# Moving the softmax's negated maximum to VectorE and the turning of queries and keys to ScalarE copies, in a two-layer diffusion step

## The chip, the core and the metric

The kernel runs on one core of one Trainium2 chip. A core has five engines with instruction queues of their own: TensorE (PE: matmuls, with PEld for its weight loads), VectorE (DVE), ScalarE (ACT), GpSimd (POOL) and SyncE (SP, which issues nearly all transfers here). The metric is the device time of one execution in microseconds (us): 2378.9 us median of three runs before the change.

## The reference

One inference step of a backbone with two layers, width 2048, for two groups of 128 tokens (context and latents). All arithmetic is fp32. Layer 0 mixes with eight heads of latent attention (A) and eight of grouped-query attention with normalised queries and keys (B); layer 1 mixes with eight heads of differential attention (C); each layer is followed by a gated ConvFFN of width 5632. What the change touches:

```
def rmsnorm(x, g):
    y = xf * lax.rsqrt(jnp.mean(xf * xf, axis=-1, keepdims=True) + EPS)
    return (y * g.astype(jnp.float32)).astype(x.dtype)

def apply_rope(x, cos, sin):
    x1, x2 = x[..., :half], x[..., half:]
    return jnp.concatenate([x1 * c - x2 * s, x1 * s + x2 * c], axis=-1)

def diff_attention(q, k, v, lam, scale):      # in each block of 128 queries
    s = jnp.einsum("bqhjd,bkhjd->bhjqk", qb, k).astype(jnp.float32) * scale
    p = jax.nn.softmax(s, axis=-1)
    a = (p[:, :, 0] - lam * p[:, :, 1]).astype(v.dtype)
    return jnp.einsum("bhqk,bkhd->bqhd", a, v)
```

Context queries see 128 context keys; latent queries see 128 cached and 128 latent keys besides, in one softmax. In C each head has two query and key halves, two softmaxes, and a norm over the head's 256 outputs times a constant.

## The kernel before

Activations lie with features on the 128 partitions and both groups' 256 tokens along the row. Every weight matrix is read once, in transfers of 1 MB (`raw`). Each is split in two parts: ACT rounds it to `wh` (L219), DVE takes the rest as `wl` (L220), and PE multiplies three times per 128x128 block: `wh` with the high and the low part of the activations (L312, L313; L298, L299 where three chunks run side by side) and `wl` with the high part (L316; L300). An output chunk of 128 features from 2048 is 48 such matmuls into one PSUM bank (`acc`, three banks). So PE, ACT and DVE all work on every weight.

The stages in order: input projection of layer 0; the heads of A and B, two per turn, beside their own weights; output projection; ConvFFN 0; then layer 1's input projection with the C heads in between, output projection `w_out_c`, ConvFFN 1.

Beside all this runs the adaLN product, 1 MB tiles `araw` of `w_ada` in two buffers. A unit of four tiles is summed either on PE (16 matmuls of 512 columns, L426, then ACT's copy `am` L368 and four transposes L375) or, for the units listed in `SUMMED`, on DVE: two instructions per tile (`junk`, L403), one per token group, each with the sum read out to `mod`. `pump(rate)` spreads these steps over the chunks. Two buffers mean that a third tile's transfer is issued when the first tile has been used.

The code is written as coroutines: `start` runs one to its first `yield`, and each `pump` lets all go one step on. The order on each engine is made from this program by a scheduler; instructions in it are then issued in order, engine by engine.

Softmax of an AB head (`head_ab`): scores to PSUM, two maxima on DVE (`mx`, L592, L593), the negated maximum times the scale on POOL (`nmx`, L597 and L598), two exponentials on ACT with their sums (`p`, L600), reciprocal and two multiplications on DVE (L624 to L626), three transposes on PE (L607), ACT's copy `pT` (L609), three matmuls with the values. A C head (`attend`) does this twice (`dmx`, POOL's L595), then DVE forms `drec` (L939), `nl` = minus lambda over the second sum (L941), multiplies the second softmax by `nl` (L943) and adds the first (L945); after the values (L952 to L954) come squares on ACT (L958), `var` on POOL (L961, the power at L963, a constant at L964), `on` on DVE (L967), four transposes (L974) and the split into `oall` (L219, L220), the input of the output projection.

A C head's `project` takes four chunks for queries and keys and two for values. For each query or key chunk ACT copies the bank to `dev` (L908) and the context tokens on to `dq` or `dk` (L909), and DVE turns the latent tokens with the helper `rope`: two products on 64 partitions crosswise (L583), one with the cosine (L585), one sum (L586).

`rstd` adds EPS on DVE (L183) and raises to the power -1/2 on POOL (L186); two of its callers then multiply by a scale on POOL (L676, L814). The residual `x` takes each output chunk on DVE (L568).

## Time and profile before

| | us |
|---|---|
| three runs | 2378.08, 2378.9, 2380.63 |
| the profiled execution | 2380.3 |
| its span (first to last instruction) | 2378.5 |
| PE busy | 2314.3 (97%) |
| DVE busy | 1810.0 (76%) |
| ACT busy | 1158.0 (49%) |
| POOL busy | 170.3 (7%) |

The profiled execution lies 1.4 us over the median of the runs and inside their spread. Times in the rows of the trace are microseconds from the start of the span; a busy share is an average over stages that have different limits, so a row for a stretch of the span says more than the table. In that count of stages the C heads run from about 1210 to 1550 us, `w_out_c` to about 1623 and the modulation of the second ConvFFN's input to about 1641.

### The profile page before, as it was taken

To read this page: it belongs to the slowest core of one execution; us is meant where nothing else is said; L and a number is where in the kernel's file an instruction comes from. 1 tells how busy PE (TensorE), PEld (TensorE's weight loads), DVE (VectorE), ACT (ScalarE), POOL (GpSimd) and SP (SyncE) were. 2 spreads that over 40 slices of the span, in tenths; PEclk is the share of its full clock that TensorE was granted. 3 is DMA by queue.
4 is the path that set the end of the run, shared out by engine and by line. 5 is a ranking of instruction groups with operands and counts; after the bars stand their busy time and mean duration, and the time that the engine had idled before them with its cause. 6 is when DMAs were issued, how large, how long until landed. Compare 5 with 4: busy or idle time off the path is not lost.

```text
span 2378.5 us, 47144 instructions
## 1 busy us (share of the span) xinstructions
PE 2314.3 (97%) x19626; PEld 2193.4 (92%) x19626; DVE 1810.0 (76%) x2685; ACT 1158.0 (49%) x1807; POOL 170.3 (7%) x205
## 2 busy tenths in 40 slices
PE   8899999999999999999999999998999999999997
PEld 6778868889999999999989999796999999999997
DVE  2667544479999999999979989898899755666654
ACT  4345544365554345554455554345555534555542
POOL 0002101110000000001220001122000000000011
PEclk9999999999999999999999999898999999999999
DMA  9886677777767877777867787686677555555553
GB/s 372 348 345 243 239 269 280 301 295 259 261 252 283 299 275 257 266 266 261 306 227 247 278 305 288 259 295 247 249 254 262 211 195 195 193 192 192 192 193 120
DMA packets 92405, 610.81 MB, mean 257 GB/s; under 512 B 9952, under 2 KB 17824, under 8 KB 20512
## 3 DMA queue, kind: packets, MB, share of 16 engines
q1 hardware_dynamic: 92192, 607.80, 69.6%
q8 instruction: 154, 2.52, 0.4%
q14 instruction: 59, 0.48, 0.1%
HBM read 603.01 MB, written 4.75 MB: 256 GB/s over the span
## 4 chain that ended last, share of the span: by engine, by line
PE 89%; DVE 5%; DMA 2%; issue 2%; ACT 1%; POOL 0%; POOLq 0%; DVEq 0%; ACTq 0%
PE acc L312 27%; PE acc L316 27%; PE acc L313 26%; PE ada L426 3%; DMA araw<-w_ada 2%; DVE junk L403 2%; DVE wl L220 2%; PE att L617 1%; PE acc L298 1%; PE acc L299 1%; PE acc L300 1%; PE misc L426 0%; PE ada L339 0%; DVE nt L515 0%; PE att L933 0%
## 5 line engine op out<-in xcount | busy, mean ns | idle before, releaser
L219 ACT CAST wh<-raw 128x1024 fp32r<-128x1024 f32 (+1 forms) x788 | 793.5, 1013 | 934.7 <-PE acc L313 765.4
L220 DVE TENSOR_TENSOR wl<-raw,wh 128x1024 fp32r<-128x1024 f32 (+1 forms) x788 | 922.0, 1185 | 344.5 <-ACT wh L219 329.5
L312 PE MATMUL acc<-hx,wh 128*128 128x256 f32 x4064 | 1130.0, 279 | 9.0 <-ACT wh L219 4.2
L316 PE MATMUL acc<-hx,wl 128*128 128x256 f32 x4064 | 1127.4, 278 | 0.9 <-DVE wl L220 0.9
L313 PE MATMUL acc<-hx,wh 128*128 128x256 f32 x4064 | 1127.0, 278 | 0.0
L312 PEld LDWEIGHTS acc<-hx,wh 128*128 128x128 f32 x4064 | 763.6, 188 | 34.2 <-issue 11.8
L316 PEld LDWEIGHTS acc<-hx,wl 128*128 128x128 f32 x4064 | 764.8, 188 | 10.3 <-issue 7.0
L313 PEld LDWEIGHTS acc<-hx,wh 128*128 128x128 f32 x4064 | 764.7, 188 | 8.8 <-issue 7.9
L403 DVE CUSTOM_DVE_ANT_0 junk<-araw,condb 128x2048 f32<-128x2048 f32 (+1 forms) x184 | 424.8, 2309 | 1.0 <-DMA araw<-w_ada 1.0
L313 PE MATMUL acc<-g,wh 128*128 128x256 f32 x1408 | 388.3, 276 | 0.0
L316 PE MATMUL acc<-g,wl 128*128 128x256 f32 x1408 | 388.0, 276 | 0.0
L312 PE MATMUL acc<-g,wh 128*128 128x256 f32 x1408 | 387.8, 276 | 0.0
L313 PEld LDWEIGHTS acc<-g,wh 128*128 128x128 f32 x1408 | 264.3, 188 | 0.0
L316 PEld LDWEIGHTS acc<-g,wl 128*128 128x128 f32 x1408 | 264.1, 188 | 0.0
L312 PEld LDWEIGHTS acc<-g,wh 128*128 128x128 f32 x1408 | 264.0, 188 | 0.0
L175 POOL TENSOR_TENSOR sqacc<-sqacc,sq 128x256 f32<-128x256 f32 x62 | 80.6, 1300 | 1528.0 <-issue 1218.9
L1012 ACT ACTIVATE cv<-acc,convw 128x256 f32<-128x256 f32 x176 | 98.3, 558 | 3.8 <-PE acc L300 3.8
L568 DVE SCALAR_TENSOR_TENSOR x<-acc,mod,x 128x128 f32<-128x128 f32 x192 | 58.0, 343 | 50.5 <-PE acc L316 49.6
L426 PE MATMUL ada<-araw,condw 128*32 128x512 f32 x608 | 83.6, 627 | 4.7 <-DMA araw<-w_ada 3.0
L1018 DVE SCALAR_TENSOR_TENSOR cv<-acc,convw,cv 128x254 f32<-128x254 f32 x176 | 84.2, 479 | 3.6
L1015 DVE SCALAR_TENSOR_TENSOR cv<-acc,convw,cv 128x254 f32<-128x254 f32 x176 | 83.5, 474 | 2.7 <-ACT cv L1012 2.7
L316 PE MATMUL acc<-oall,wl 128*128 128x256 f32 x208 | 57.6, 277 | 1.2 <-DVE wl L220 1.2
(230 smaller groups left out, 1820.9 us busy)
## 6 DMA issues: line engine op xcount, KB each, us to landing
araw<-w_ada SPq DMA_DIRECT2D x186, 1024.0 KB, 5.3
raw<-w_up SPq DMA_DIRECT2D x176, 1024.0 KB, 4.8
raw<-w_down SPq DMA_DIRECT2D x88, 1024.0 KB, 4.8
raw<-w_in_c SPq DMA_DIRECT2D x48, 1024.0 KB, 6.0
raw<-w_in_ab SPq DMA_DIRECT2D x19, 1024.0 KB, 7.0
raw<-w_out_ab SPq DMA_DIRECT2D x16, 1024.0 KB, 7.1
raw<-w_out_c SPq DMA_DIRECT2D x16, 1024.0 KB, 5.9
raw<-w_ada SPq DMA_DIRECT2D x6, 1024.0 KB, 10.5
```

Source lines behind the costliest of these rows:

```text
L175: pool.tensor_tensor(out=st["acc"], in0=st["acc"], in1=sq, op=ALU.add)
L219: pin(act.copy(out_hi, src))
L220: pin(dve.tensor_tensor(out=out_lo, in0=src, in1=out_hi.bitcast(F32), op=ALU.subtract))
L312: fixed(pe.matmul(ps[:, :n], wh, xh(k), start=(i == 0), stop=False))
L313: fixed(pe.matmul(ps[:, :n], wh, xl(k), start=False, stop=False))
L316: fixed(pe.matmul(ps[:, :n], wl, xh(k), start=False, stop=(i == last)))
L403: tc.keep_in_program_order(dve.tensor_tensor_reduce(out=junk, in0=raw, in1=condb[:, c].rearrange("p (g n) -> p g n", g=4), scale=1.0, scal ...
L426: i = pe.matmul(ada["ps"][32 * g:32 * g + 32, :], condw[:, 4 * t + g, :], raw[:, g], start=(t == 0), stop=(t == 3), skip_group_check=True)
L568: dve.scalar_tensor_tensor(out=x[:, c, s], in0=ps[:, s], scalar=mod[:, l, 3 * which + 2, c, g:g + 1], in1=x[:, c, s], op0=ALU.mult, op1=AL ...
L1012: pin(act.activation(y, ps, AF.Identity, scale=cw[:, 1, m:m + 1], bias=cw[:, 3, m:m + 1]))
L1015: pin(dve.scalar_tensor_tensor(out=y3[:, :, 1:], in0=p3[:, :, :T - 1], scalar=cw[:, 0, m:m + 1], in1=y3[:, :, 1:], op0=ALU.mult, op1=ALU.add))
L1018: pin(dve.scalar_tensor_tensor(out=y3[:, :, :T - 1], in0=p3[:, :, 1:], scalar=cw[:, 2, m:m + 1], in1=y3[:, :, :T - 1], op0=ALU.mult, op1=A ...
```

## The change

Five edits.

1. `rstd` takes a factor, and DVE's addition of EPS multiplies by factor to the power -2 in the same instruction. The two multiplications by a scale on POOL (L676 once, L814 eight times) go; the power stays.
2. `softmax_parts` makes `nmx` in one DVE instruction instead of one or two on POOL, in all 16 AB heads and 16 times in C.
3. In `project`, the copy `dev` of queries and keys goes. ACT copies three times from the PSUM bank: 64 latent partitions crosswise to each half of `dsh` (two buffers) and the context tokens to `dq` or `dk`. DVE multiplies the bank by the cosine, `dsh` by the sine table, and subtracts (the table's halves differ only in sign). The bank is now held until DVE's product.
4. The multiplication of the second softmax by `nl` goes from DVE to ACT.
5. `var` is made on DVE instead of POOL, with the constant inside; POOL keeps the power.

```diff
-    def rstd(cols, n):
+    def rstd(cols, n, factor=1.0, out=None):
...
-            dve.tensor_scalar(out=v[:, at:at + w], in0=ps, scalar1=EPS, scalar2=None, op0=ALU.add)
+            dve.tensor_scalar(out=v[:, at:at + w], in0=ps, scalar1=EPS, scalar2=factor ** -2,
+                              op0=ALU.add, op1=ALU.mult)
...
-            pool.tensor_scalar(out=nmx, in0=mx, scalar1=-const, scalar2=None, op0=ALU.mult)
+            dve.tensor_scalar(out=nmx, in0=mx, scalar1=-const, scalar2=None, op0=ALU.mult)
         else:
-            pool.tensor_scalar(out=nmx, in0=mx, scalar1=-1.0, scalar2=None, op0=ALU.mult)
-            pool.tensor_tensor(out=nmx, in0=nmx, in1=rs, op=ALU.mult)
+            dve.scalar_tensor_tensor(out=nmx, in0=mx, scalar=-1.0, in1=rs, op0=ALU.mult, op1=ALU.mult)
...
-                        rq = stat_rstd(sq, 768)
-                        pool.tensor_scalar(out=rsm, in0=rq[:, 0:2], scalar1=MLA_SCALE,
-                                           scalar2=None, op0=ALU.mult)
+                        stat_rstd(sq, 768, factor=MLA_SCALE, out=rsm)
...
-                    r = rstd([pst[:, 0:2]], 2)
-                    pool.tensor_scalar(out=rsb[:, h], in0=r[:, 0:2], scalar1=HEAD_SCALE,
-                                       scalar2=None, op0=ALU.mult)
+                    rstd([pst[:, 0:2]], 2, HEAD_SCALE, rsb[:, h])
...
-                    ev = T_(cp, [P, NT], "dev", bufs=2)
-                    act.copy(ev, product())
-                    act.copy(dst[:, i, 0:T], ev[:, 0:T])
-                    rope(dst[:, i:i + 1, to:], ev[:, None, T:], 1, 64, "rch", "rsh")
+                    ps = product()
+                    sh = T_(cp, [P, T], "dsh", bufs=2)
+                    act.copy(sh[64:], ps[:64, T:])
+                    act.copy(sh[:64], ps[64:, T:])
+                    act.copy(dst[:, i, 0:T], ps[:, 0:T])
+                    turned = dst[:, i, to:to + T]
+                    dve.tensor_tensor(out=turned, in0=ps[:, T:], in1=C("rch"), op=ALU.mult)
+                    dve.tensor_tensor(out=sh, in0=sh, in1=C("rsh"), op=ALU.mult)
+                    dve.tensor_tensor(out=turned, in0=turned, in1=sh, op=ALU.subtract)
...
-                dve.tensor_scalar(out=pj[1][:, ks], in0=pj[1][:, ks], scalar1=nl[:, g:g + 1],
-                                  scalar2=None, op0=ALU.mult)
+                act.activation(pj[1][:, ks], pj[1][:, ks], AF.Identity, scale=nl[:, g:g + 1])
...
-            pool.tensor_scalar(out=var, in0=ss, scalar1=1.0 / 256, scalar2=EPS,
-                               op0=ALU.mult, op1=ALU.add)
+            k2 = (1.0 - LAMBDA_INIT) ** -2
+            dve.tensor_scalar(out=var, in0=ss, scalar1=k2 / 256, scalar2=k2 * EPS,
+                              op0=ALU.mult, op1=ALU.add)
             pool.tensor_tensor(out=var, in0=var, in1=C("mhalf")[:, 0:2], op=ALU.pow)
-            pool.tensor_scalar(out=var, in0=var, scalar1=1.0 - LAMBDA_INIT, scalar2=None,
-                               op0=ALU.mult)
```

The scheduler orders every engine anew. Three places matter below; the lines of the changed kernel lie one further down around here (the `junk` of L403 stands at L404, the `wl` of L220 at L221, PE's L426 at L427).

VectorE, an AB head in the first half of the heads, before: the maxima, a weight's split, and then the reciprocal and the two products, with a second weight behind them.

```order
L592 TENSOR_REDUCE mx_2887<-att_2884 128x1
L593 TENSOR_REDUCE mx_2887<-att_2884 128x1
L220 TENSOR_TENSOR wl_3276<-raw_3273,wh_3275 128x1024
L624 RECIPROCAL rec_2897<-sums_2888 128x2
L625 TENSOR_SCALAR p_2889<-p_2889,rec_2897 128x128
L626 TENSOR_SCALAR p_2889<-p_2889,rec_2897 128x256
L220 TENSOR_TENSOR wl_3280<-raw_3273,wh_3279 128x1024
```

The same head after:

```order
L593 TENSOR_REDUCE mx_2875<-att_2872 128x1
L594 TENSOR_REDUCE mx_2875<-att_2872 128x1
L598 SCALAR_TENSOR_TENSOR nmx_2878<-mx_2875,rsb_238 128x2
L624 RECIPROCAL rec_2884<-sums_2876 128x2
L625 TENSOR_SCALAR p_2877<-p_2877,rec_2884 128x128
L626 TENSOR_SCALAR p_2877<-p_2877,rec_2884 128x256
L221 TENSOR_TENSOR wl_3255<-raw_3252,wh_3254 128x1024
```

`nmx` now stands right behind the maxima, and the weight's split that stood between maxima and reciprocal is behind the products.

VectorE at the end of C, the last head's second softmax, before (`mod` is a sum's read-out, `dmx` the maxima, `drec` and `nl` the reciprocals and the factor, `p` the softmaxes):

```order
L592 TENSOR_REDUCE dmx_18044<-att_18056 128x1
L593 TENSOR_REDUCE dmx_18044<-att_18056 128x1
L403 ISA junk_17642,mod_77<-araw_17527,condb_82 128x2048
L403 ISA mod_77 128x1
L939 RECIPROCAL drec_18066<-dsums_18045 128x4
L403 ISA junk_17644,mod_77<-araw_17527,condb_82 128x2048
L403 ISA mod_77 128x1
L941 TENSOR_SCALAR nl_18068<-drec_18066,nlam_14347 128x2
L385 TENSOR_TENSOR mod_77<-mod_77,cst_74 128x8
L943 TENSOR_SCALAR p_2662_18059<-p_2662_18059,nl_18068 128x128
L943 TENSOR_SCALAR p_2662_18059<-p_2662_18059,nl_18068 128x256
L945 SCALAR_TENSOR_TENSOR p_2659_18049<-p_2659_18049,drec_18066,p_2662_18059 128x128
```

And after:

```order
L404 ISA junk_17575,mod_77<-araw_17459,condb_82 128x2048
L404 ISA mod_77 128x1
L221 TENSOR_TENSOR oall_14316<-att_17725,oall_14316 128x2x256
L593 TENSOR_REDUCE dmx_17971<-att_17983 128x1
L594 TENSOR_REDUCE dmx_17971<-att_17983 128x1
L596 TENSOR_SCALAR nmx_17977<-dmx_17971 128x2
L386 TENSOR_TENSOR mod_77<-mod_77,cst_74 128x8
L596 TENSOR_SCALAR nmx_17987<-dmx_17971 128x2
L940 RECIPROCAL drec_17993<-dsums_17972 128x4
L942 TENSOR_SCALAR nl_17995<-drec_17993,nlam_14313 128x2
L945 SCALAR_TENSOR_TENSOR p_2618_17976<-p_2618_17976,drec_17993,p_2621_17986 128x128
L945 SCALAR_TENSOR_TENSOR p_2618_17976<-p_2618_17976,drec_17993,p_2621_17986 128x256
```

The two `junk` that stood around the reciprocal are ahead of the last maxima now; between the maxima and `p` there is none. By count the unit before it is also finished earlier: the next `junk` that DVE has after this place, one of the following unit, stands ahead of the first residual `x` (L569), where before it stood behind those of three chunks and two weights.

TensorE at the same place, before: the last three units' matmuls (`ada`) around the head's transposes (L607), values (L952 to L954) and output transposes (L974).

```order
L426 MATMUL ada_17806<-araw_17728,condw_79 32x512 x4
L607 MATMUL att_18074<-cst_74,p_2659_18049 128x128 x3
L952 MATMUL att_18080<-dv_17566,pT_18078 128x256
L953 MATMUL att_18080<-dv_17566,pT_18078 128x256
L954 MATMUL att_18080<-dv_17566,pT_18078 128x256
L426 MATMUL ada_17806<-araw_17804,condw_79 32x512 x4
L426 MATMUL ada_17806<-araw_17811,condw_79 32x512 x4
L974 MATMUL att_18094<-cst_74,on_18085 128x128 x4
L298 MATMUL acc_18107<-oall_14350,wh_18122 128x256
```

And after:

```order
L427 MATMUL ada_17734<-araw_17732,condw_79 32x512 x4
L607 MATMUL att_18001<-cst_74,p_2618_17976 128x128 x3
L952 MATMUL att_18007<-dv_17498,pT_18005 128x256
L953 MATMUL att_18007<-dv_17498,pT_18005 128x256
L954 MATMUL att_18007<-dv_17498,pT_18005 128x256
L427 MATMUL ada_17734<-araw_17739,condw_79 32x512 x4
L427 MATMUL ada_17734<-araw_17811,condw_79 32x512 x4
L973 MATMUL att_18020<-cst_74,on_18012 128x128 x4
L376 MATMUL ada_17953<-cst_74,am_17888 128x128 x4
L299 MATMUL acc_18033<-oall_14316,wh_18048 128x256
```

The rows read alike, but they name other tiles: before, the tile ahead of L607 is the first of its unit and the fourth comes 18 output matmuls after L974; after, it is the second, so the whole unit stands ahead of L973 and its transposes right behind.

More of the change, by code (lines that the diff above doesn't have):

```diff
@@ L182, in rstd @@
             w = n // len(cols)
-            dve.tensor_scalar(out=v[:, at:at + w], in0=ps, scalar1=EPS, scalar2=None, op0=ALU.add)
+            dve.tensor_scalar(out=v[:, at:at + w], in0=ps, scalar1=EPS, scalar2=factor ** -2,
+                              op0=ALU.add, op1=ALU.mult)
             at += w
-        r = T_(small, [P, 2], "rr")
+        r = T_(small, [P, 2], "rr") if out is None else out
         pool.tensor_tensor(out=r[:, :n], in0=v[:, :n], in1=C("mhalf")[:, :n], op=ALU.pow)
@@ L193, in att_bank, with stat_rstd @@
         return T_(ppool["att"], [P, 512], "att", bufs=3)
-    def stat_rstd(st, width, bank=bank):
+    def stat_rstd(st, width, bank=bank, **kw):
         ps = bank()
@@ L200, in stat_rstd @@
             pe.matmul(ps[:, g:g + 1], st["last"][:, t], inv(width), start=False, stop=True)
-        return rstd([ps[:, 0:2]], 2)
+        return rstd([ps[:, 0:2]], 2, **kw)
     def diagonal(r, cols):
```

## The prediction

> **What bounds the kernel now.** I read the page first, then the stretches by stage, then PE's waits, then the chain at the places where PE waits.
>
> ```profile
> PE 2314.3 (97%) x19626; PEld 2193.4 (92%) x19626; DVE 1810.0 (76%) x2685; ACT 1158.0 (49%) x1807; POOL 170.3 (7%) x205
> L220 DVE TENSOR_TENSOR wl<-raw,wh 128x1024 fp32r<-128x1024 f32 (+1 forms) x788 | 922.0, 1185 | 344.5 <-ACT wh L219 329.5
> ```
>
> PE is busy for all but 64.2 us of the span, and the change removes nothing from PE; so the most it can give is a part of PE's idle time. The stretches say where that idle time lies (columns: stretch, length, busy PE, PEld, DVE, ACT, POOL, granted clock, DMA share, GB/s).
>
> ```profile
> 612.00:1206.00 594.00, 592.72 (x5232) 592.64 (x5230) 544.39 (x679) 289.39 (x378) 25.18 (x14) 1.00 0.73 269
> ...
> 1412.00:1530.00 118.00, 115.63 (x980) 112.92 (x978) 115.61 (x177) 59.39 (x119) 15.18 (x16) 1.00 0.78 285
> 1530.00:1550.00 20.00, 16.07 (x78) 8.38 (x78) 10.10 (x22) 5.59 (x17) 3.31 (x4) 0.66 0.66 243
> 1550.00:1623.00 73.00, 71.80 (x631) 71.25 (x628) 72.16 (x87) 31.80 (x47) 15.70 (x13) 1.00 0.79 287
> 1623.00:1640.00 17.00, 5.97 (x26) 2.80 (x28) 14.85 (x26) 5.60 (x11) 2.69 (x4) 0.60 0.68 265
> ```
>
> In the ConvFFN (612 to 1206) PE is full: nothing to gain. From 1412 PE and DVE are both full to 98%, while ACT has half its time free. At 1530 to 1550, the end of the last C head, PE has idle time and a clock of 0.66. In `w_out_c` both are full again, and behind it (1623 to 1640) DVE alone is: PE waits for DVE's last residuals and `junk`. So C's end is a matter of DVE's queue, and a shorter DVE queue counts there once, at the tail. The waits of PE (total, times, longest) in the AB heads, 300 to 380:
>
> ```profile
> PE att L607 <- DVE p L625: 3.2, 3, 1.4
> PE ada L375 <- ACT am L368: 1.1, 1, 1.1
> ```
>
> And at the tail, 1510 to 1645:
>
> ```profile
> PE att L607 <- DVE p L945: 1.6, 1, 1.6
> ```
>
> **The AB heads.** One softmax chain of them:
>
> ```profile
> 340.82 0.34 DVE mx L593
> 341.31 0.22 POOL nmx L597
> 341.61 0.21 POOL nmx L598
> 341.84 1.10 ACT p L600 x4
> ```
>
> From the end of `mx` (341.16) to the exponentials it takes 0.68 us. After, one DVE instruction of two columns stands there; the trace has no such `nmx` on DVE, and the nearest row is L183's (below), 0.155 us, with as little between steps again: about 0.2 us, 0.5 us saved per chain. PE's idle time on these chains is 3.2 us in three waits plus 1.1 us on `am`, which ACT copies in the same queue. Three waits shortened by 0.5 us are 1.5 us; the reordered DVE row, where a weight's split moves behind the products, can take another 1.185 us from a wait, and what a wait loses another transfer can take back. I take -1.7 us, between 0 and -3.5. The nine POOL multiplications by a scale and the folded factor cost DVE nothing, the instruction being there already; they lie ahead of the heads, and no wait of PE in the rows is on them: 0.
>
> **The C heads.** The prices, by the groups of the trace:
>
> ```profile
> L585 DVE TENSOR_TENSOR dk<-dev,cst x16: 274/285/293, 1236.7 to 1505.1; 128x128 f32<-128x128 f32 x16
> L583 DVE TENSOR_TENSOR rope<-dev,cst x64: 284/286/290, 1233.2 to 1519.1; 64x128 f32<-64x128 f32 x64
> L943 DVE TENSOR_SCALAR p<-p,nl x16: 278/316/352, 1256.2 to 1536.7; 128x128 f32<-128x128 f32 x8, 128x256 f32<-128x256 f32 x8
> L183 DVE TENSOR_SCALAR rv<-misc x14: 148/155/160, 20.1 to 2365.7; 128x2 f32<-128x2 f32 x13, 128x1 f32<-128x1 f32 x1
> L908 ACT COPY dev<-acc x32: 357/365/403, 1231.8 to 1501.2; 128x256 f32<-128x256 f32 x32
> L518 ACT ACTIVATE nt<-nt,mod,scl x64: 477/491/498, 30.1 to 1652.4; 128x128 f32<-128x128 f32 x64
> ```
>
> DVE per head: four turnings lose one crosswise product each (4 x 0.286 = 1.14) and the two products by `nl` go (2 x 0.316 = 0.63); two `nmx` and one `var` come (3 x 0.155 = 0.47). Net -1.3 us. The product from PSUM and the one from `dsh` are priced like L583, as they replace products of that length; bounds 0.25 and 0.42 us, which is 0.5 us per head either way. ACT per head: four times three copies for two, at 0.365 as the upper price (+1.5), and two multiplications, at most 0.491 each (+1.0): +2.5 us at most of the 34 us that a head's six chunks take on PE (288 matmuls at 115.63 us / 980), on an engine half idle; covered by that idle time. If it weren't, `wh` would be late, and with it PE: that is rival C.
>
> From 1412 DVE's row is full, so its savings are time. The new order, however, puts two more `junk` (2.2 us each) ahead of the last maxima. Adding DVE's instructions from 1413.9 to those maxima by the durations of their rows gives 116.5 us before and 115.5 us after, the savings of 5.5 us (1.3 for each of some four heads) less 4.5 us: the maxima end at 1529.7 instead of 1530.7. Then the tail:
>
> ```profile
> 1530.39 0.34 DVE dmx L593
> ...
> 1530.80 2.20 POOL nmx L595
> ...
> 1533.02 0.92 ACT p L600 x4
> ...
> 1533.97 0.18 DVE drec L939
> 1534.15 2.18 DVE junk L403
> ...
> 1536.54 0.15 DVE p L943
> 1536.70 7.13 DMA araw<-w_ada
> 1543.87 1.45 PE ada L426 x8
> ...
> 1545.34 7.57 DMA araw<-w_ada
> ```
>
> Of the timelines of POOL, DVE and PE, rows beside that chain (start, duration; in brackets the idle time before and what ended it), and the six transfers of `araw` issued between 1524 and 1556:
>
> ```profile
> 1529.68 0.21 POOL L595 TENSOR_SCALAR nmx<-dmx 128x2 f32<-128x2 f32 x1 [4.87 <-DVE dmx L593]
> ```
>
> ```profile
> 1530.64 2.28 DVE L403 CUSTOM_DVE_ANT_0 junk<-araw,condb 128x2048 bf16<-128x2048 f32 x1
> ...
> 1536.98 0.74 DVE L945 SCALAR_TENSOR_TENSOR p<-p,drec,p 128x128 f32<-128x128 f32 x2
> 1544.24 0.88 DVE L967 SCALAR_TENSOR_TENSOR on<-att,var,cst 128x256 f32<-128x256 f32 x2 [6.52 <-POOL var L964]
> 1548.13 1.18 DVE L568 SCALAR_TENSOR_TENSOR x<-acc,mod,x 128x128 f32<-128x128 f32 x4 [0.93 <-PE acc L300]
> ```
>
> ```profile
> 1545.20 0.66 PE L974 MATMUL att<-cst,on 128*128 128x128 f32 x4
> ```
>
> ```profile
> DMA to landing us min/median/max: 4.8/5.5/7.6
> ```
>
> POOL's two-column `nmx` took 0.21 us beside short DVE work and 2.20 us beside a `junk`: that is what the last chain pays for, with another 2.18 us for the `junk` ahead of `nl`. Both go. From 1529.7: `nmx` 0.2, the exponentials 0.95, `drec` and `nl` 0.35, the product by `nl` on ACT 0.9 (two at 0.49 less overlap), the sums 0.6 to 0.75: `p` at about 1533.6, 4.1 us ahead of the 1537.72 of before.
>
> This isn't what the output gets. PE's queue has a tile of adaLN (L426) ahead of the transposes and three of that unit ahead of `on`'s transposes, and in a ring of two buffers a tile is issued when the one before last has been used. Such a transfer took 7.13 and 7.57 us in the chain, beside another, and 4.8 at the least. The first one is issued when DVE's last `junk` ahead of the maxima ends (about 1528.6) and lands at 1533.5 to 1534.5; its matmuls, and the transposes of `p` end 1.0 to 2.0 us later than `p` allows. That leaves 2 to 2.9 us of the 4.1. `on` follows at the same distance (values, squares, `var`, power), at 1541.9 to 1542.8; the unit's last tile lands at 1540 to 1542, and L974 begins at 1541.9 to 1543.1 instead of 1545.20: 2.1 to 3.3 us. `var` on DVE saves the two short POOL steps, 0.4 us, and is in this.
>
> Next late is the residual: a `junk` of the following unit now stands ahead of the first `x`, its tile lands at 1546 to 1548.5, and 2.3 us later the residuals begin, at 1548.2 to 1550.7, against 1548.13: up to here the gain is spent. But this `junk` is no longer behind them, which with the wait of before it (0.84 us) is 3.1 us less of DVE's full queue until 1633. Together -3.0 to -0.5 us at the end of C; I take the middle, -1.9.
>
> **Sum.** -1.7 (AB) -1.9 (C's tail) = -3.6 us on the profiled execution's 2380.3, which lies 1.4 us over the median of the runs: 2376.7 there, 2375.3 as a median. What a measurement of this kernel tells from no change is 0.2%, 4.8 us: the forecast lies just inside.
>
> [...] VectorE here reads the cosine product from PSUM. [...]
>
> ```profile
> L755 DVE TENSOR_TENSOR proj<-proj,acc x60: 407/420/424, 67.8 to 205.7; 128x256 f32<-128x256 f32 x60
> ...
> L1035 DVE TENSOR_TENSOR cv<-cv,cv x88: 414/422/426, 505.0 to 2247.1; 128x256 f32<-128x256 f32 x88
> ```
>
> A product or sum with one operand in PSUM (L755) takes 420 ns, one from SBUF alone (L1035) 422; I keep the row.
>
> **Rivals.** A: the transfers don't bind. They land after 4.8 us, the fastest of the six, and PE's queue follows `p` and `on`: 4.1 us earlier, 2.3 spent on the `junk` ahead, 3.1 saved behind, -4.9 in C; with -2 to -3.5 in AB the sum is -6.9 to -8.4, the median 2371.3. For it speaks that PE needs 1.45 us for the eight rows of matmuls on landed tiles; against it the 7 us transfers.
>
> B: hidden. The transfers take 7.6 us, the following unit's `junk` stands until 1551.8 ahead of the residuals, and C gives +0.6 to 0: with AB's -1.7 at best, 2377 to 2379.5. The two DMA rows speak for it.
>
> C: slower, by DVE's queue itself. `nmx` now stands in order behind whatever DVE does, a `junk` and a weight (2.28 + 1.185 = 3.5 us), and the exponentials, `nl`, and ACT's product wait for it, in heads where POOL was free to answer at once. PE's L607 in heads 0 to 6 found `p` ready before (no wait of PE on it there but the last head's 1.6). By counting rows the new order has the transposes 6 to 7 us earlier among PE's matmuls, and leaves 1.6 to 2.3 us between `p` and its reader. This decides from a lateness of 2.3 us: at 3.5 us each of seven heads would cost 1.2 us, +8.4, less the -3.6: 2383.7. The same holds for a bank of `acc`, held until the cosine product: the last `dk` was copied at 1501.2 and multiplied at 1505.1 (the rows of L908 and L585), a lag of 3.9 us, and of three banks one is wanted again after two chunks, 11 us; only a lag more than twice as long would stop PE. Against C speaks that the rows of DVE are moved together with the chain.
>
> **Chances.** Forecast 0.41, its own range 2372.5 to 2378.5 (the terms' ends, -6.5 to -0.5; a third of it over 4.8 us faster); A 0.28; B 0.11; C 0.20. Faster by over 0.2%: A and 0.14 of the forecast, 0.42. Within: the other 0.27 of the forecast, B, and 0.02 of C, 0.40. Slower: 0.18. The range goes from A's fast end, 2370, to C at its price, 2384.
>
> **What the profile after would show.** Right: no POOL `nmx`; L607's waits in the AB heads under 3.2 us by about 1.5; the last maxima near 1528 (AB's gain included), `p` 4 us behind them; PE then waiting for `araw`, not for `p`; the modulation of the second ConvFFN beginning 3 to 4 us earlier; the ConvFFNs unchanged to 1 us. Wrong: waits of L607 on `p` or of `acc` on a late bank inside heads 0 to 6, `wh` late on ACT, or PE idle between 1412 and 1530 over the 2.4 us of before. Another order of transfers at the tail alone would move the result between A and B.

## The result and the profile after

The changed kernel takes 2377.16 us (median of 12 runs, 2374.52 to 2381.42) against 2380.2 us of the kernel before in the same series: a ratio of 0.9989 with a 95% interval of 0.998 to 0.9997. A second series on another occasion gave 2377.03 against 2381.12, 0.998 (0.9971 to 0.9989). So it is 3 to 4 us faster, at or under the 0.2% that the prediction took as the least that a measurement tells from no change, but clear of noise in both series; the forecast was -3.6 us. The time itself, 2377.16 us, lies in the forecast's own range and also at the fast end of rival B's (2377 to 2379.5), so it is the stretches below that decide between them.

The page of the changed kernel, its first part:

```profile
PE 2315.6 (98%) x19626; PEld 2196.9 (93%) x19626; DVE 1799.1 (76%) x2677; ACT 1172.7 (49%) x1855; POOL 136.6 (6%) x132
```

VectorE has 11 us less to do, ScalarE 15 us more, GpSimd 73 instructions less; TensorE does the same work. The waits of TensorE in the AB heads (300 to 380) are now:

```profile
PE att L607 <- DVE p L625: 1.4, 2, 0.8
PE acc L313 <- ACT hx L220: 0.5, 1, 0.5
```

One softmax chain there, from the chain of work that ended last (the same head as in the prediction):

```profile
338.65 0.34 DVE mx L594
...
339.02 0.17 DVE nmx L598
...
339.22 1.11 ACT p L600 x4
```

From the end of the maxima to the exponentials it is 0.23 us instead of 0.68. The end of the C heads, waits of TensorE between 1505 and 1641:

```profile
PE att L201 <- ACT sq L171: 3.9, 1, 3.9
PE misc L427 <- DMA araw<-w_ada: 2.8, 1, 2.8
PE acc L313 <- DVE x L569: 2.3, 1, 2.3
PE ada L427 <- DMA araw<-w_ada: 2.2, 1, 2.2
```

No wait on `p` is left; TensorE waits for an adaLN tile, and later for the residual. The chain shows it in order of time:

```profile
1525.85 0.65 PE att L934 x4
...
1527.92 4.75 DMA araw<-w_ada
...
1532.71 1.94 PE ada L427 x8
1534.65 0.85 PE att L607 x3
...
1538.98 2.17 PE ada L427 x16
...
1541.16 6.45 DMA araw<-w_ada
...
1547.64 0.35 DVE x L569
```

And VectorE's timeline beside it:

```profile
1528.55 0.42 DVE L594 TENSOR_REDUCE dmx<-att 128x1 f32<-128x256 f32 x1
1528.88 0.16 DVE L596 TENSOR_SCALAR nmx<-dmx 128x2 f32<-128x2 f32 x1
...
1531.80 0.88 DVE L945 SCALAR_TENSOR_TENSOR p<-p,drec,p 128x128 f32<-128x128 f32 x2 [0.53 <-ACT p L944]
...
1545.16 2.29 DVE L404 CUSTOM_DVE_ANT_0 junk<-araw,condb 128x2048 bf16<-128x2048 f32 x1 [1.11 <-DMA araw<-w_ada]
...
1547.38 1.12 DVE L569 SCALAR_TENSOR_TENSOR x<-acc,mod,x 128x128 f32<-128x128 f32 x4
```

`p` is ready at 1532.68, but its transposes (L607) wait until 1534.65 for a tile's matmuls (eight rows of the trace); and the `junk` of the next unit, waiting for its own tile, stands ahead of the residual.

**How kernels are compared below.** Profiles can't be compared by their end: TensorE's order is the same in every kernel here up to the first matmul of the AB heads' query weights, and that matmul began between 219.8 us and 226.0 us in the profiles of this study. I take stretches instead: AB from that matmul to the start of ConvFFN 0's last residual, C from there to the start of ConvFFN 1's last residual. For the kernel before, the AB stretch is 983.5 us (221.15 to 1204.61) and the C stretch 1159.3 us (1204.61 to 2363.88).

| kernel | median us, its kernel before | ratio (95%) | AB stretch | C stretch |
|---|---|---|---|---|
| before | | | 983.5 | 1159.3 |
| changed | 2377.16, 2380.2 | 0.9989 (0.998 to 0.9997) | 981.6 | 1158.0 |
| after_again | 2377.03, 2381.12 | 0.998 (0.9971 to 0.9989) | 981.2 | 1156.8 |
| ab_only | 2378.99, 2381.12 | 0.9995 (0.9986 to 1.0004) | 981.5 | 1159.6 |
| c_only | 2380.21, 2381.12 | 0.9999 (0.999 to 1.0008) | 984.4 | 1157.7 |
| no_turn | 2378.1, 2381.12 | 0.9989 (0.998 to 0.9997) | 981.7 | 1160.5 |
| turn | 2377.27, 2380.41 | 0.9986 (0.9976 to 0.9996) | 983.2 | 1156.8 |
| nl_act | 2379.43, 2380.41 | 1.0 (0.9991 to 1.0009) | 984.9 | 1160.7 |
| nmx_c | 2387.59, 2380.41 | 1.0026 (1.0014 to 1.0038) | 982.9 | 1169.2 |
| after_quarter | 2380.46, 2380.41 | 1.0011 (0.9985 to 1.0036) | 982.0 | 1162.7 |
| ab_turn | 2374.94, 2381.86 | 0.996 (0.9927 to 0.9994) | 983.4 | 1155.7 |
| nmx_turn | 2386.48, 2381.86 | 1.002 (1.0011 to 1.0029) | 984.1 | 1164.2 |
| ab_turn_pe31 | 2369.54, 2381.86 | 0.9952 (0.9939 to 0.9964) | 981.7 | 1151.6 |
| nmx_turn_nl | 2378.79, 2381.93 | 0.9985 (0.9976 to 0.9995) | 985.3 | 1157.7 |

Two profiles of the changed kernel differ by 0.4 us in the AB stretch and 1.2 us in the C stretch; that is the grain of the table. Every other kernel has one profile, so a difference of 1 to 1.5 us between two rows says little. "Changed" and "after_again" are the same program; by TensorE's order `c_only` has the changed kernel's C part, `ab_only` that of the kernel before, and `ab_turn` that of `turn`.

### The profile page after: what moved, and what is told of

It is laid out like the page before. It is cut to its first block, busy times and chain, and to the rows that moved or that the text cites. A ratio compares the mean times of both kernels' runs of the same rounds, so it can differ in the third digit from the quotient of the medians.

```text
span 2374.0 us, 47094 instructions
## 1 busy us (share of the span) xinstructions
PE 2315.6 (98%) x19626; PEld 2196.9 (93%) x19626; DVE 1799.1 (76%) x2677; ACT 1172.7 (49%) x1855; POOL 136.6 (6%) x132
## 4 chain that ended last, share of the span: by engine, by line
PE 95%; DVE 2%; DMA 1%; issue 1%; ACT 1%; POOL 0%; POOLq 0%; DVEq 0%; ACTq 0%
PE acc L313 28%; PE acc L317 28%; PE acc L314 28%; PE ada L427 3%; DMA araw<-w_ada 1%; PE att L617 1%; PE acc L300 1%; PE acc L299 1%; PE acc L301 1%; PE misc L427 0%; PE att L934 0%; PE att L607 0%; DVE wl L221 0%; PE ada L340 0%; PE ada L376 0%
## 5 line engine op out<-in xcount | busy, mean ns | idle before, releaser
L220 ACT CAST wh<-raw 128x1024 fp32r<-128x1024 f32 (+1 forms) x788 | 794.0, 1013 | 943.1 <-PE acc L314 775.7
L221 DVE TENSOR_TENSOR wl<-raw,wh 128x1024 fp32r<-128x1024 f32 (+1 forms) x788 | 923.0, 1186 | 343.8 <-ACT wh L220 324.5
L404 DVE CUSTOM_DVE_ANT_0 junk<-araw,condb 128x2048 f32<-128x2048 f32 (+1 forms) x184 | 424.8, 2309 | 1.1 <-DMA araw<-w_ada 1.1
L569 DVE SCALAR_TENSOR_TENSOR x<-acc,mod,x 128x128 f32<-128x128 f32 x192 | 58.0, 343 | 49.2 <-PE acc L317 49.2
L427 PE MATMUL ada<-araw,condw 128*32 128x512 f32 x608 | 83.2, 624 | 6.0 <-DMA araw<-w_ada 5.0
L313 PE MATMUL acc<-oall,wh 128*128 128x256 f32 x208 | 58.4, 281 | 2.3 <-DVE x L569 2.3
```

Of the source, the lines that this page charges most:

```text
L220: pin(act.copy(out_hi, src))
L221: pin(dve.tensor_tensor(out=out_lo, in0=src, in1=out_hi.bitcast(F32), op=ALU.subtract))
L313: fixed(pe.matmul(ps[:, :n], wh, xh(k), start=(i == 0), stop=False))
L404: tc.keep_in_program_order(dve.tensor_tensor_reduce(out=junk, in0=raw, in1=condb[:, c].rearrange("p (g n) -> p g n", g=4), scale=1.0, scal ...
L427: i = pe.matmul(ada["ps"][32 * g:32 * g + 32, :], condw[:, 4 * t + g, :], raw[:, g], start=(t == 0), stop=(t == 3), skip_group_check=True)
L569: dve.scalar_tensor_tensor(out=x[:, c, s], in0=ps[:, s], scalar=mod[:, l, 3 * which + 2, c, g:g + 1], in1=x[:, c, s], op0=ALU.mult, op1=AL ...
```

## The experiments

**The two halves, and the changed kernel again.** By its order, `ab_only` is the changed kernel until the end of ConvFFN 0 and the kernel before from there on; `c_only` is the reverse. So the halves can be cut without changing what the other part of the program does.

`ab_only`: the norms' factors and the AB heads' negated maximum alone.

```diff
-            pool.tensor_scalar(out=nmx, in0=mx, scalar1=-1.0, scalar2=None, op0=ALU.mult)
-            pool.tensor_tensor(out=nmx, in0=nmx, in1=rs, op=ALU.mult)
+            dve.scalar_tensor_tensor(out=nmx, in0=mx, scalar=-1.0, in1=rs, op0=ALU.mult, op1=ALU.mult)
...
-                    r = rstd([pst[:, 0:2]], 2)
-                    pool.tensor_scalar(out=rsb[:, h], in0=r[:, 0:2], scalar1=HEAD_SCALE,
-                                       scalar2=None, op0=ALU.mult)
+                    rstd([pst[:, 0:2]], 2, HEAD_SCALE, rsb[:, h])
```

> The kernel before with the norms' factors and the AB heads' negated maximum on VectorE alone; differential attention as before. By its order it is the changed kernel up to the end of ConvFFN 0 and the kernel before from there on. Theory (the AB heads carry the larger part, as the two profiles read: 3.2 of 4.5 us): 2 to 3.5 us faster than before, the last residual of the AB output projection 4 to 5 us earlier and the first third of that given back at the modulation behind it. Rival 1 (the prediction's sum, -1.7 and -1.9): 1.7 us faster. Rival 2 (the two profiles differ by chance in this part, the AB chains were hidden): within 0.7 us of before, L607's waits in the heads as before.

Measured: a ratio of 0.9995, whose interval holds 1; the medians differ by 2.1 us. The stretches decide more finely. From the first query matmul to the last head's product with the values, the seven profiles with AB's edits take 153.21 to 153.45 us and the seven without 155.63 to 157.10: 2.7 us of means. Over the whole AB stretch the means are 981.9 and 984.0, a gain of 2.2 us: the rest is given back at the modulation behind the output projection, where in the changed order the sums of two adaLN tiles stand ahead of ConvFFN 0's first products and wait for both tiles (0.80 and 0.56 us, where before there was one wait of 0.90). Rival 2 (chance) falls; the theory and rival 1 are not told apart by 0.5 us. The last residual of the AB output projection came 2.4 us earlier by the clock (3.2 counted from the first query matmul), not the 4 to 5 us that the theory had.

`c_only`: the four edits of differential attention alone (its negated maximum, the turning, `nl` on ScalarE, `var` on VectorE).

```diff
-            pool.tensor_scalar(out=nmx, in0=mx, scalar1=-const, scalar2=None, op0=ALU.mult)
+            dve.tensor_scalar(out=nmx, in0=mx, scalar1=-const, scalar2=None, op0=ALU.mult)
...
-                    ev = T_(cp, [P, NT], "dev", bufs=2)
-                    act.copy(ev, product())
...
+                    ps = product()
+                    sh = T_(cp, [P, T], "dsh", bufs=2)
...
+                act.activation(pj[1][:, ks], pj[1][:, ks], AF.Identity, scale=nl[:, g:g + 1])
...
+            dve.tensor_scalar(out=var, in0=ss, scalar1=k2 / 256, scalar2=k2 * EPS,
+                              op0=ALU.mult, op1=ALU.add)
```

> The kernel before with the three edits of differential attention and its negated maximum on VectorE alone; the AB heads as before. Theory (C's tail gives what the transfers leave, as the profiles read: 1.3 us): 0.5 to 2 us faster. Rival 1 (the prediction's term): 1.9 us. Rival 2 (the whole tail chain counts): 4 to 5 us. Rival 3 (lost again in the order of the adaLN tiles): no faster than before.

The time is not to be told from that of before (0.9999), the C stretch is 1.6 us shorter. With the two profiles of the changed kernel (1.3 and 2.5 us) the mean is 1.8 us. Rival 2 falls; against rival 3 (no faster than before) speak the stretches alone, the run times don't exclude it.

`after_again`: the changed kernel once more.

> The changed kernel once more, on the same chip as the three others. All theories: 2 to 4 us faster than before. If the gains of its two halves add, its gain is the sum of the two halves' within 1 us. Its profile tells how far two profiles of one kernel differ at the stages' ends: expected under 1 us.

4.1 us faster; the halves' medians give 2.1 + 0.9 = 3.0, which is 1.1 us apart and so just outside the 1 us expected. The two profiles of the same program differ by 1.2 us in the C stretch, slightly more than I expected, and all of it behind the last maxima: TensorE waited 2.2 us for tiles there in one and 5.2 in the other. The one that waited longer for tiles has the shorter stretch, so these waits alone don't set it.

**Which edit of C does it.** `no_turn` is the changed kernel with the turning undone:

```diff
-                    ps = product()
-                    sh = T_(cp, [P, T], "dsh", bufs=2)
...
+                    ev = T_(cp, [P, NT], "dev", bufs=2)
+                    act.copy(ev, product())
+                    act.copy(dst[:, i, 0:T], ev[:, 0:T])
+                    rope(dst[:, i:i + 1, to:], ev[:, None, T:], 1, 64, "rch", "rsh")
```

> The changed kernel with the turning of queries and keys undone (copy, and four products and sums on VectorE). If VectorE's shorter queue matters in C (0.286 us less for each of 32 turnings, about 4 of 8 heads where VectorE is full, so 4 to 5 us before the tail): the last maxima 3 to 5 us later than in the changed kernel and the time 0.5 to 3 us longer. If only the negated maximum and the product by nl at the tail matter: as the changed kernel within 0.7 us.

The C stretch is 2.5 to 3.7 us longer than in the changed kernel, and 1.2 us longer than before. The run times don't resolve this: 2378.1 us against 2377.03 in the same series, with intervals that overlap, and the same median lies 3.0 us under the kernel before. The last maxima are not later: 327.1 us after the stretch's start in both. By the ends of the stages, 1.1 to 2.7 us are lost between the maxima and the first residual, and 1.1 to 1.5 us behind the output projection. There is a wait ahead of the maxima too (waits of TensorE between 1505 and 1650):

```profile
PE att L968 <- DVE on L961: 2.7, 1, 2.7
```

With the turning back on VectorE, the seventh head's `var` runs there 3.6 us after the squares were done, behind a `junk` and two weights; its power on GpSimd takes 2.59 us beside the next `junk`, and TensorE waits 2.7 us for `on`.

`turn` is the reverse, the kernel before with the turning alone.

> The kernel before with only the turning by crosswise copies. Theory (it is the largest of VectorE's savings, 1.14 us in each of some four full heads, and undoing it in the changed kernel lengthened the stretch by 2.5 to 3.7 us): the last maxima 3 to 5 us earlier, and the stretch 1157 to 1158.5, the GpSimd step and the sum ahead of nl still in the tail. Rival (the tail with its GpSimd step takes all back): 1159 to 1160. Rival (ScalarE's three copies or the held bank cost): over 1160.5, with TensorE waiting for wh or for a bank in the heads.

The runs say 0.9986, the stretch 1156.8 us, 2.5 us under before: by itself the turning gives what all four edits of C give together. Again the last maxima are where they were (325.6 us after the stretch's start, 325.7 before), so the theory's way there is wrong although its time is right. In this order the split into `oall` stands ahead of a `junk` and of the last maxima; TensorE's wait of 2.1 us for `oall`, which the kernel before has at 1528, is gone, and the first residual follows the maxima by 15.6 us instead of 17.8. That is 2.2 of the 2.5 us, and it is a matter of this order as much as of the edit.

`nl_act` is the kernel before with the product by `nl` on ScalarE alone.

```diff
-                dve.tensor_scalar(out=pj[1][:, ks], in0=pj[1][:, ks], scalar1=nl[:, g:g + 1],
-                                  scalar2=None, op0=ALU.mult)
+                act.activation(pj[1][:, ks], pj[1][:, ks], AF.Identity, scale=nl[:, g:g + 1])
```

> The kernel before with only the product of the second softmax by nl on ScalarE. Theory (VectorE loses 0.63 us in each of some four heads in which it is full, less what two more adaLN sums ahead of the chain take): the stretch 1158 to 1159.5. Rival (ScalarE's product is late behind its weights, over 1 us from nl to the sums): over 1160.

No gain (1.0), a stretch 1.4 us longer, hardly more than the grain. ScalarE wasn't late (it began its product 0.0 to 0.9 us after `nl`); TensorE waited 4.9 us for adaLN tiles at the tail, in three waits. The rival had the number, not the reason.

`nmx_c` is the kernel before with C's negated maximum on VectorE alone (the first pair of lines in `c_only`'s diff).

> The kernel before with only differential attention's negated maximum on VectorE. From the last residual of ConvFFN 0 to that of ConvFFN 1, before: 1159.3 and 1159.6 us. Theory (the 2.2 us of GpSimd at the tail are on the chain, 0.3 us per head come to VectorE, the rest is order): 1157.5 to 1159. Rival (all of C's gain is this one edit, 1.3 to 2.5 us): 1156.8 to 1158. Rival (a late negated maximum behind VectorE's queue costs in all heads): over 1160.5, with waits of L607 on p in heads 0 to 6.

This one is slower, by 0.26% (0.14 to 0.38%), 7.2 us by the medians and 10.0 us in the stretch of its profile. The mechanism looks like the prediction's rival C, at a place that it had not named. TensorE's waits from 1205 to 1560:

```profile
PE att L974 <- DVE on L967: 8.6, 2, 4.4
```

And VectorE's queue ahead of the second of these:

```profile
1530.71 0.74 DVE L945 SCALAR_TENSOR_TENSOR p<-p,drec,p 128x128 f32<-128x128 f32 x2
1531.37 2.35 DVE L220 TENSOR_TENSOR wl<-raw,wh 128x1024 fp32r<-128x1024 f32 x2
1533.64 2.28 DVE L403 CUSTOM_DVE_ANT_0 junk<-araw,condb 128x2048 bf16<-128x2048 f32 x1
1535.85 1.22 DVE L220 TENSOR_TENSOR wl<-raw,wh 128x1024 fp32r<-128x1024 f32 x1
1536.99 2.28 DVE L403 CUSTOM_DVE_ANT_0 junk<-araw,condb 128x2048 bf16<-128x2048 f32 x1
...
1540.45 0.88 DVE L967 SCALAR_TENSOR_TENSOR on<-att,var,cst 128x256 f32<-128x256 f32 x2 [1.17 <-POOL var L964]
```

`p` came late, everything behind it late, and TensorE stood still for `on`. The last thing that `on` waited for was `var`, still on GpSimd: 2.9 us from the end of the squares, with VectorE idle for the last 1.17 us. Whether the late `p` or the slow `var` is to blame this run doesn't tell; `nmx_turn_nl` below bears on it. How much room the chain has is seen in the time from the end of `p` to the transposes that read it, in heads 0 to 6: at least 1.6 us in the kernel before, 2.1 (up to 4.8) in the changed one, 0.0 in `nmx_c`.

`nmx_turn` adds the turning to `nmx_c`, to see whether a shorter queue heals it.

> The kernel before with C's negated maximum on VectorE and the turning, the AB heads as before. The negated maximum alone cost 9.8 us in the stretch, by the waits of the output transposes on on. Theory (a queue of VectorE that is full, and on and p standing behind its sums and weights; the turning takes 1.14 us per head off that queue): the waits of 4 us on on go, and the stretch is 1156.5 to 1159. Rival (the order with the negated maximum on VectorE is late whatever the load): 1162 to 1169 as without the turning.

It doesn't: 1164.2 us, 0.2% slower than before (0.11 to 0.29%). The rival holds. The chain of the seventh head in VectorE's timeline, in order, with the steps of one of its two softmaxes and most of the sums between them:

```profile
1513.18 0.41 DVE L593 TENSOR_REDUCE dmx<-att 128x1 f32<-128x256 f32 x1
...
1513.59 2.28 DVE L403 CUSTOM_DVE_ANT_0 junk<-araw,condb 128x2048 bf16<-128x2048 f32 x1
...
1515.80 0.16 DVE L595 TENSOR_SCALAR nmx<-dmx 128x2 f32<-128x2 f32 x1
...
1520.95 2.28 DVE L403 CUSTOM_DVE_ANT_0 junk<-araw,condb 128x2048 bf16<-128x2048 f32 x1
...
1524.30 0.17 DVE L944 RECIPROCAL drec<-dsums 128x4 f32<-128x4 f32 x1
...
1525.50 2.28 DVE L403 CUSTOM_DVE_ANT_0 junk<-araw,condb 128x2048 bf16<-128x2048 f32 x1
...
1527.71 0.22 DVE L946 TENSOR_SCALAR nl<-drec,nlam 128x2 f32<-128x2 f32 x1
1527.84 2.28 DVE L403 CUSTOM_DVE_ANT_0 junk<-araw,condb 128x2048 bf16<-128x2048 f32 x1
...
1531.19 0.54 DVE L948 TENSOR_SCALAR p<-p,nl 128x128 f32<-128x128 f32 x2
1531.65 2.28 DVE L403 CUSTOM_DVE_ANT_0 junk<-araw,condb 128x2048 bf16<-128x2048 f32 x1
...
1533.86 0.74 DVE L950 SCALAR_TENSOR_TENSOR p<-p,drec,p 128x128 f32<-128x128 f32 x2
```

Steps of 0.2 to 0.7 us, and ahead of nearly each a `junk` of 2.28 us, with weights in the gaps: TensorE then waited 5.5 us for this `p` and 3.5 for its `on`. There is no room left in this head: the transposes begin behind the first part of `p`, 0.3 us before its second part is done.

`nmx_turn_nl` takes the products by `nl` off this chain.

> As nmx_turn, and the product of the second softmax by nl on ScalarE; only var is still on GpSimd, otherwise differential attention is that of the changed kernel. nmx_turn's stretch between the two ConvFFNs' last residuals was 1164.2 us, with all four of C's edits it was 1156.8 to 1158.0. Theory (the softmax chain of a head visits VectorE's full queue once less with nl's products on ScalarE, so p is 2 us or more ahead of its reader again): 1157 to 1159.5, no wait of L607 on p in heads 0 to 6. Rival (var on GpSimd, stretched to 1.7 to 2.6 us beside the sums, is what holds on back): 1161 to 1165, with waits of the output transposes on on of 3 to 4 us.

1157.7 us and 0.9985: healed, no wait on `p` or `on` in heads 0 to 6, a slack of 2.1 to 3.7 us there, with `var` still on GpSimd; so the rival that `var` holds `on` back falls. In the last head TensorE still waits 3.5 us for `p`. So in C the negated maximum on VectorE and the product on ScalarE need each other, in these orders: the one adds a visit to VectorE's queue, the other takes a visit away. Every edit also makes the scheduler draw a new order for all engines; what an order does and what an edit does can't be separated further with these runs.

**The transfers at the tail.** In `after_quarter` three of the four tiles that TensorE waits for at the last head are loaded to a quarter.

```diff
+            if ada["i"] == 29 and t:
+                tile_ = ada["raw"]
+                sp.dma_start(out=tile_[:, 0], in_=A["w_ada"][l, j, q, t, :, 0])
+                ada["raw"] = {(slice(None), k): tile_[:, 0] for k in range(4)}
+            else:
+                sp.dma_start(out=ada["raw"], in_=A["w_ada"][l, j, q, t])
```

> The changed kernel, in which the second to fourth adaLN tile of the unit that TensorE sums at the last C head are loaded to a quarter only (its matmuls run on that quarter four times; the part left out is three quarters of these tiles, and the modulation of one unit is not the reference's). Theory (the transfers gate the last head's transposes in the changed kernel: TensorE waited 2.2 and 5.2 us for them in its two profiles): L607 follows the softmax within 0.3 us, no wait on araw ahead of the output transposes, the last residual of the output projection 1 to 3 us earlier; from the last residual of ConvFFN 0 to that of ConvFFN 1, 1155 to 1157 us against 1158.0 and 1156.8. Rival (VectorE's full queue behind is the limit, and what the transfers give is lost to the adaLN sums ahead of the residuals): the waits on araw go, and the stretch stays at 1156.8 to 1158.

Both expectations failed: the stretch is 1162.7 us, 5 us longer than the changed kernel's. The transposes follow `p` within 0.3 us, as the theory said, but TensorE still waits 2.6 us for the unit's last tile ahead of the output transposes, and then elsewhere for longer (waits between 1505 and 1650, then GpSimd's timeline):

```profile
PE att L978 <- DVE on L971: 5.9, 1, 5.9
```

```profile
1548.51 2.60 POOL L969 TENSOR_TENSOR var<-var,cst 128x2 f32<-128x2 f32 x1 [26.51 <-DVE var L967]
```

In the new order a step that waits for TensorE's transposes of that unit, and a `junk`, stand ahead of `var`, which in the changed kernel is VectorE's. `var` ran 2.0 us after the squares were done, the power on GpSimd took 2.60 us beside the next `junk` (0.69 us in the changed kernel's last head, at 1540.20, where VectorE was idle), and `on` was late. So the run doesn't show what the transfers cost, which stays open; it shows that `var` on VectorE has the weakness of rival C too.

**Two more versions, the second of which beats both.** `ab_turn` keeps the AB edits and the turning and leaves the other three edits of C away.

> The kernel before with the AB heads' edits and the turning alone: the negated maximum of differential attention, the product by nl and var stay where they were. Theory (the turning carries C's whole gain, 2.5 us of the stretch between the two ConvFFNs' last residuals, and the other three edits of C give nothing or cost): AB's 2.0 and C's 2.5 add to 4.5 us, 0.5 to 1 us under the changed kernel. Rival (the tail needs the negated maximum on VectorE and nl on ScalarE as well): 1 us over the changed kernel, TensorE waiting for p in the last head.

2374.94 us, a ratio of 0.996 (0.9927 to 0.9994); the C stretch is the shortest so far, 1155.7 us, with the wait of 2.7 us on `p` that the rival had expected. The AB stretch shows no gain in this profile (983.4): the 2.9 us gained in the heads were lost again at the modulation and in ConvFFN 0. That `ab_turn` is faster than the changed kernel is not shown: the intervals overlap, and the two stretches together, 2139.0 us, lie between those of the changed kernel's two profiles (2139.6 and 2138.0).

`ab_turn_pe31` also gives the last of the adaLN units that VectorE sums to TensorE:

```diff
-SUMMED = [22, 23, 24, 26, 27, 28, 30, 31]
+SUMMED = [22, 23, 24, 26, 27, 28, 30]
```

> As ab_turn, with the last of the eight adaLN units that VectorE sums given to TensorE: eight sums of 2.2 us less on VectorE behind the C heads, some 2.3 us more on TensorE. Theory (VectorE is the limit behind the heads: its last sums end 3 us after its last residual, and TensorE idles 11 of 17 us there): 1 to 4 us under ab_turn. Rival (TensorE is as full there): 1 to 3 us over ab_turn.

2369.54 us, 0.9952 (0.9939 to 0.9964): 12 us under before by medians, and clear of the changed kernel; 5.4 us under `ab_turn`, more than the 1 to 4 expected, of which 4.1 are in the C stretch. The stretches 1550 to 1623 and 1623 to 1640 (columns as in the prediction), first of `ab_turn`:

```profile
1550.00:1623.00 73.00, 69.34 (x607) 68.75 (x605) 73.00 (x87) 31.06 (x44) 17.77 (x13) 1.00 0.79 292
1623.00:1640.00 17.00, 8.86 (x36) 4.65 (x37) 14.74 (x29) 6.76 (x15) 3.82 (x6) 0.51 0.56 218
```

And of `ab_turn_pe31`:

```profile
1550.00:1623.00 73.00, 71.72 (x624) 67.78 (x622) 58.40 (x78) 32.06 (x45) 15.46 (x12) 1.00 0.78 293
1623.00:1640.00 17.00, 15.52 (x105) 10.63 (x104) 14.46 (x36) 11.91 (x27) 7.67 (x10) 0.90 0.48 186
```

VectorE is no longer full in the output projection, and TensorE, which idled half of the last 17 us, works through most of them at a clock of 0.90 instead of 0.51. The windows are fixed in time and `ab_turn_pe31` is 5.4 us ahead at the last residual (1621.2 against 1626.7), so its last row holds some of the next stage's work; but its waits say the same: between the last residual and the second ConvFFN TensorE waits 3.0 us for the norm's sums on GpSimd (`sqacc`), 3.7 for ScalarE's squares (`sq`) and 3.3 for an adaLN tile in `ab_turn`, and 1.3 us for the squares alone of these in `ab_turn_pe31`.

## Why the prediction was right, and where its steps were not

**AB, -1.7 us forecast: right.** Measured over the stretch -2.2 us of means. The parts: L607's waits from 3.2 to 1.4 us (-1.8; forecast 1.5), the wait of 1.1 us on `am` gone, 0.45 us per chain (forecast 0.5); then some of it given back at the modulation, which the forecast had only as "another transfer can take back". `nmx` on VectorE took 0.160 us, priced 0.155.

**C, -1.9 us forecast: right in sum** (-1.3, -2.5 and, without AB's edits, -1.6), with one step wrong, and in part by luck. Parts of the C stretch, from its start to the last maxima, to the first residual behind the heads, to the last residual of the output projection:

| | to the maxima | to the first x | to the last x |
|---|---|---|---|
| before | 325.7 | 17.8 | 81.6 |
| changed, two profiles | 327.1, 327.2 | 18.8, 17.2 | 78.4, 78.4 |

- The step "from 1412 VectorE's row is full, so its savings are time", by which the maxima were to come 1.0 us earlier, failed: they come 1.4 us later. The maxima need the last head's scores, and what stands ahead of these is TensorE's: 2680 rows of matmuls from the start of the stretch, as many in both kernels. In the kernel before TensorE's only wait over 0.15 us between 1240 and 1528 is one of 0.4 us, so VectorE's savings had nothing to shorten there. The same 118 us in the changed kernel (counted from the start of C, which is 3.2 us earlier), and ScalarE's and VectorE's waits in them:

```profile
1408.80:1526.80 118.00, 118.00 (x1007) 117.09 (x1005) 113.28 (x165) 63.05 (x127) 3.98 (x3) 1.00 0.79 286
```

```profile
ACT wh L220 <- PE acc L314: 32.7, 23, 2.3
```

```profile
DVE wl L221 <- ACT wh L220: 4.1, 5, 1.3
```

  VectorE, with less to do, waits 4.1 us for `wh`, which ScalarE can't write before TensorE is done with its buffer. The 2.4 us that TensorE idles in the prediction's row for the kernel before lie almost all behind the last scores, in its wait for `oall`. The changed kernel shortens that wait; before, and after:

```profile
PE acc L299 <- DVE oall L220: 2.1, 1, 2.1
```

```profile
PE acc L300 <- DVE oall L221: 0.6, 1, 0.6
```

  The last scores themselves end 325.1 us after the start of the stretch instead of 323.2. That is TensorE's doing, though its waits up to there add up to only 0.3 us more: between 40 and 315 us after the start, one weight matmul starts 115.0 ns behind the other on average, where they follow directly, in the changed kernel's two profiles and in `c_only`, and 113.9 ns in the kernel before, `ab_only`, `turn` and `nmx_turn_nl`. Over some 2000 of them that is 2.3 us. What makes these steps longer stays open. Neither undoing nor isolating the turning moved the maxima earlier; in `ab_turn`, `ab_turn_pe31` and `nmx_turn_nl`, which have the turning, they come 1.0, 0.8 and 1.7 us earlier than before, which no run here explains. The sign "the last maxima near 1528" came out at 1529.0 by the clock only because AB's gain and an earlier start of the heads had moved the whole C stretch forward by 3.2 us.
- The tail chain was right: from the end of the maxima to the end of `p` 3.7 us instead of 7.0, in both profiles (forecast 3.9, although the terms that it lists add up to 3.2 at most). The tile's matmuls then hold L607 back by 1.9 us in one profile and 1.0 in the other (forecast 1 to 2).
- The residual starts 2.4 and 0.8 us later after the start of the stretch than before, inside the forecast's 0.1 to 2.6, and the output projection behind it is 3.2 us shorter (forecast 3.1): the `junk` that moved ahead is gained back there, as was said.
- That the residual came out in its range is luck: the maxima ended 2.4 us later in the stretch than forecast (327.5 us instead of 325.1), and from there to the first residual it took 18.4 and 16.8 us, where the forecast had 18.5 to 21.0. The two errors took each other back. The middle of the forecast's -3.0 to -0.5, besides, is -1.75 and not -1.9.

**The prices.** ScalarE's copies from PSUM took 0.258, 0.263 and 0.266 us, under the 0.365 taken as the upper price, and its product by `nl` 0.463 us: 1.4 us per head, not 2.5. The cover held; ScalarE had 63 of 118 us to do there.

**A source in PSUM.** The changed kernel has both forms side by side, of one shape:

```profile
L909 DVE TENSOR_TENSOR dq<-acc,cst x16: 278/284/286, 1229.6 to 1491.5; 128x128 f32<-128x128 f32 x16
```

```profile
L910 DVE TENSOR_TENSOR dsh<-dsh,cst x32: 278/285/293, 1229.4 to 1501.7; 128x128 f32<-128x128 f32 x32
```

284 ns (`dq`, L909) with one operand in PSUM, 285 (`dsh`, L910) without: no difference for this operation in this kernel, as in the rows L755 and L1035 by which the prediction kept its price (420 and 422 ns).

**The rivals.** A (the transfers don't bind) did not happen: TensorE waited 2.2 and 5.2 us for tiles. B (hidden) did not either, with 1.3 to 2.5 us in C. C did not happen in the changed kernel; that it stayed away because `nl`'s product had left VectorE's chain is what `nmx_turn` and `nmx_turn_nl` suggest. It did happen in its neighbours: in `nmx_turn`, it seems in `nmx_c`, and by `var` and `on` in `no_turn` and `after_quarter`. My chance of 0.20 was for the mechanism at `p`; the stalls came as much at `on`, one step later.

## What to carry to other kernels

A short step that was moved into a full queue cost here not its 0.16 us but the instructions that the schedule put ahead of it, a `junk` of 2.28 us at a time in `nmx_turn`; count how often a chain visits that queue before and after, not how long its steps are. When two engines stand at 98% in one stretch, first look where each of them still waits: here TensorE waited 0.4 us in 288, so taking work off VectorE could not bring the last scores forward. The gain was to be had where one of them was full alone, as behind the C heads, where taking one unit of sums off VectorE gave about as much as all five edits (4.1 us in the C stretch, against 3.1 and 4.8 in both stretches together for the edits).

## What the runs showed that I had not expected

- GpSimd's steps of two columns took very different times. In the kernel before, one `nmx` of the last head took 0.21 us (at 1529.68, beside a step of VectorE of 0.68 us) and the other 2.19 us (at 1530.80, beside a `junk` of 2.28). In the changed kernel the power took 0.69 us where VectorE was idle (at 1540.20) and 2.60 us beside a `junk` of 2.28 (at 1425.26). What makes the steps longer there, no run here shows.
- The first 220 us vary by up to 6 us from run to run, while the AB heads' stretch of 153.3 us repeats within 0.24 us over the seven profiles with AB's edits, and within 1.5 us over the seven without: a stage's own length is a sharper measure than the end of the span.
- The single edits of C don't add: the turning -2.5, `nl` +1.4 and the negated maximum +10.0 us in the stretch, against -1.3 to -2.5 for all of them; each of the three is one profile of one order.
